# A 32-byte skew between operand chunks and weight slots in SBUF, in a two-block float32 network on one core

## The chip, the core and the metric

The kernel runs on one core of a Trainium2 chip. The metric is the device time of one execution in microseconds. Three timed executions of the kernel before gave 1040.45, 1042.25 and 1042.31 us; the median is 1042.25 us. [...]

## What is computed

Two transformer blocks follow each other on 256 tokens of 1,024 features, in float32. The first has a gated feed-forward layer, a mixer (neighbourhood attention on a grid, and pooling over windows), a second feed-forward layer and a gate; the second has a mixer (stick-breaking attention and a convolution), an attention over 256 memory tokens, and a third feed-forward layer. Nearly all arithmetic is in products of the 256 tokens with weight matrices:

```python
def swiglu(x, w_gate, w_up, w_down):
    return (jax.nn.silu(x @ w_gate) * (x @ w_up)) @ w_down
...
f = swiglu(rms_norm(h, ffn1_pre_g[i]), ffn1_w_gate[i], ffn1_w_up[i], ffn1_w_down[i])
h = h + 0.5 * rms_norm(f, ffn1_post_g[i])
m = hybrid_mixer(rms_norm(h, mix_pre_g[i]), w_in[i], rpb[i], pool_w[i], pool_scale[i],
                 w_br_attn[i], w_br_pool[i], w_out[i])
...
x = x + memory_cross_attention(rms_norm_2(x, norm_mem_q[l]), rms_norm_2(mem, norm_mem_kv[l]),
                               w_mem_q[l], w_mem_kv[l], w_mem_o[l])
hf = rms_norm_2(x, norm_ffn[l])
gate, up = jnp.split(hf @ w_ffn_in[l], 2, axis=-1)
x = x + (jax.nn.silu(gate) * up) @ w_ffn_out[l]
```

## The kernel before

**Tiles.** Features lie on partitions, tokens along the partition. An operand of 1,024 features is a tile of 8 chunks of 128 features, each chunk 256 float32 values (1,024 bytes) per partition. Every operand is held as two tiles of type float32r, a high part (H) and a low part (L), and every product of a 128 by 128 weight block with a chunk is three matmuls into the same PSUM bank (`mm3`, line 187): H chunk with high weights, H chunk with low weights, L chunk with high weights. The chunk (256 columns) is the moving operand, the weight block the stationary one. So the order on TensorE is, for each block, (xH, wh), (xH, wl), (xL, wh), and all of these matmuls carry the line of the helper, L184.

**Weights.** `Stream` (line 50) brings the weights in 345 units of 8 blocks, in the order in which TensorE takes them. A unit is 1,024 values (4,096 bytes) per partition. SyncE loads it into one of 5 slots of `raw`; ScalarE casts it into one of 7 slots of `wh` (line 90); VectorE subtracts that from `raw` into one of 6 slots of `wl` (line 101). `take` (line 105) hands out the blocks, 512 bytes apart within a slot.

**Stages.** Moving operands are `xH`, `xL` (the normed stream, 5,280 matmuls of 256 columns), `aH`, `aL` (22 chunks, the gated hidden layer of the three feed-forward layers, 1,584 matmuls), and smaller ones: `oH`, `oL`, `yH`, `yL` (branches of the mixers), `mH`, `mL` (memory), `x2H`, `x2L`, `moH`, `moL`, `pH`, `pL`. In the memory attention `xH` and `xL` hold the keys, `mvH` and `mvL` the values; they are filled from DRAM by GpSimd's transfers `kv` (line 1081). In the first products of each mixer (`first_group`) the weights move (512 columns) and slices of `xH` and `xL` are stationary.

**Order.** It is written out by hand: closures due after so many ticks (`after`, `tick`), generators of half tasks, and fillers for the norms. No scheduler moves anything.

**Places in SBUF.** Tiles stand one behind the other in the order in which the pools and tiles are made, in steps of 32 bytes. From the sizes in the code, counted in bytes within a partition: GpSimd's descriptor ring 0 to 16,384, then 128 bytes of constants, `hg` at 16,512, `xH` at 25,184, `xL` at 33,376, `fg`, then small tiles, `raw` from 52,032, `wh` from 72,512, `wl` from 101,184, `aH` at 141,536 and `aL` at 164,064; `mH`, `mL` (later `x2H`, `x2L`) from 212,960 up to the end. Slots of `wh` and `wl` are 4,096 bytes apart, blocks 512, chunks 1,024: all of them multiples of 512. So the place of an operand modulo 512 is the same for every chunk of a tile and for every weight block:

| operand | place mod 512 before | moving less stationary, mod 512 |
|---|---|---|
| every block of `wh`, `wl` | 320 | |
| `xH`, `xL` with weights | 96 | 288 |
| `aH`, `aL`, `oH`, `oL`, `yH`, `yL`, `moH`, `moL` with weights | 224 | 416 |
| `mH`, `mL`, `x2H`, `x2L` with weights | 480 | 160 |
| `xH`, `xL` (keys) with queries | 96 with 224 | 384 |
| `pH`, `pL` (probabilities) with `mvH`, `mvL` | 224 with 224 | 0 |

I call the last column the distance of a matmul's two operands. Lines that the change touches:

```python
h = self.hl.tile([P, UB * P], F32R, tag="wh", name="wh", bufs=HL_BUFS + 1)   # lines 73, 88
l = self.hl.tile([P, UB * P], F32R, tag="wl", name="wl")                     # lines 74, 100
self.xH = b.tile([P, DC, T], F32R, name="xH")                                # line 211
aH = fp.tile([P, FC, T], F32R, name="aH")                                    # line 409
nc = bacc.Bacc("TRN2", target_bir_lowering=False, num_devices=1)             # line 1402
```

## Time and profile before

| | |
|---|---|
| timed executions | 1040.45, 1042.25, 1042.31 us |
| span of the profiled execution, first to last instruction | 1040.2 us |
| what lies around the span, up to the median (the profiled execution has no time of its own beside its span) | 2.0 us |
| TensorE busy with matmuls | 1030.7 us (99%), 8,606 records |
| TensorE busy with weight loads | 1022.6 us (98%), 8,606 records |
| VectorE, ScalarE, GpSimd busy | 709.6, 545.7, 44.0 us |
| DMA queues: SyncE's, GpSimd's | 53.6% and 1.8% of 16 engines' span |

Matmul records overlap each other (one lasts 280 ns, the next starts some 117 ns later), so TensorE's busy time says little. What says how fast it goes is the distance from one start to the next. The chain of waits gives it: a piece "PE mm L184 xN" of so many microseconds is N matmuls that follow each other without a wait, and the quotient is the time that one takes.

### The profile page before, as it was taken

Reading aid. Unit: us, or ns where it says so; the run is one execution under the profiler, and the core shown is the slowest. Engines: PE = TensorE matmul, PEld = TensorE weight load, DVE = VectorE, ACT = ScalarE, POOL = GpSimd, SP = SyncE. Lnnn points to the kernel's source line nnn. Section 1 sums busy time; section 2 is a strip of 40 time slices with the busy share of each in tenths; the row PEclk is TensorE's granted clock in tenths of the full one; section 3 lists DMA queues with packets and bytes.
Section 4 is the critical chain, followed back from the end, with each engine's and each line's share of the span. In section 5 each row is a group of like instructions: output and inputs, shape, how many; then the busy total and the mean of one; then the engine's idle time right before and its main releaser. Section 6 shows DMA issues by size and latency. Waiting matters only on the chain.

```text
span 1040.2 us, 20720 instructions
## 1 busy us (share of the span) xinstructions
PE 1030.7 (99%) x8606; PEld 1022.6 (98%) x8606; DVE 709.6 (68%) x1062; ACT 545.7 (52%) x857; POOL 44.0 (4%) x73
## 2 busy tenths in 40 slices
PE   9999999999999999999999999999999999999997
PEld 8999999999999999999999999999999999999996
DVE  7777754587858677666447776886678677666642
ACT  7655544464644555454446565465556555544431
POOL 0100000120000110000000111000001000000000
PEclk9999999999999999999999999999999999999999
DMA  8765564555545655556555666454566346555541
GB/s 287 244 214 181 194 215 171 181 190 185 194 151 166 229 179 193 184 191 190 196 167 177 195 201 194 159 168 157 160 222 226 110 139 219 187 199 182 178 147 42
DMA packets 55023, 191.50 MB, mean 184 GB/s; under 512 B 6400, under 2 KB 7936, under 8 KB 54928
## 3 DMA queue, kind: packets, MB, share of 16 engines
q1 hardware_dynamic: 52992, 184.37, 53.6%
q0 software_dynamic: 1936, 5.80, 1.8%
q8 instruction: 67, 1.10, 0.4%
q14 instruction: 28, 0.23, 0.1%
HBM read 187.00 MB, written 3.15 MB: 183 GB/s over the span
## 4 chain that ended last, share of the span: by engine, by line
PE 81%; issue 16%; DMA 1%; DVE 1%; SPq 0%; POOL 0%; POOLq 0%; DVEq 0%; ACT 0%
PE mm L184 77%; PE at L184 3%; DMA raw<-ws 1%; PE at L839 1%; DMA hg<-gx 0%; DVE sqp L315 0%; POOL r L264 0%; DVE wl L79 0%; SPq L63 0%; DVE wl L101 0%; DVE xL L290 0%; DVE fg L1323 0%; POOLq L1405 0%; DVEq L1405 0%; ACT wh L78 0%
## 5 line engine op out<-in xcount | busy, mean ns | idle before, releaser
L184 PE MATMUL mm<-xH,wh 128*128 128x256 f32 x1760 | 494.9, 281 | 0.0
L184 PE MATMUL mm<-xH,wl 128*128 128x256 f32 x1760 | 492.2, 280 | 0.8 <-DVE wl L79 0.4
L184 PE MATMUL mm<-xL,wh 128*128 128x256 f32 x1760 | 491.4, 279 | 0.0
L101 DVE TENSOR_TENSOR wl<-raw,wh 128x1024 fp32r<-128x1024 f32 x340 | 405.8, 1218 | 22.0 <-ACT wh L90 7.4
L90 ACT CAST wh<-raw 128x1024 fp32r<-128x1024 f32 x340 | 350.2, 1046 | 53.0 <-PE mm L184 33.5
L184 PEld LDWEIGHTS mm<-xH,wl 128*128 128x128 f32 x1760 | 331.2, 188 | 2.6 <-DVE wl L79 1.4
L184 PEld LDWEIGHTS mm<-xH,wh 128*128 128x128 f32 x1760 | 331.3, 188 | 1.6 <-ACT wh L78 0.8
L184 PEld LDWEIGHTS mm<-xL,wh 128*128 128x128 f32 x1760 | 331.1, 188 | 0.0
L184 PE MATMUL mm<-aH,wh 128*128 128x256 f32 x528 | 148.9, 282 | 0.0
L184 PE MATMUL mm<-aL,wh 128*128 128x256 f32 x528 | 148.2, 281 | 0.0
L184 PE MATMUL mm<-aH,wl 128*128 128x256 f32 x528 | 148.2, 281 | 0.0
L415 ACT ACTIVATE z<-z 128x256 f32<-128x256 f32 x66 | 27.2, 418 | 145.6 <-DVE z L414 145.5
L184 PEld LDWEIGHTS mm<-aH,wl 128*128 128x128 f32 x528 | 99.6, 189 | 0.0
L184 PEld LDWEIGHTS mm<-aH,wh 128*128 128x128 f32 x528 | 99.6, 189 | 0.0
L184 PEld LDWEIGHTS mm<-aL,wh 128*128 128x128 f32 x528 | 99.5, 189 | 0.0
L414 DVE TENSOR_TENSOR z<-mm,rs 128x512 f32<-128x512 f32 x66 | 44.7, 689 | 77.5 <-PE mm L184 71.8
L305 DVE TENSOR_TENSOR acc<-acc,sq 128x256 f32<-128x256 f32 x27 | 11.5, 425 | 65.0 <-ACT sq L304 64.9
L264 POOL TENSOR_TENSOR r<-v,mhalf 128x2 f32<-128x2 f32 x13 | 17.6, 1355 | 685.7 <-DVE v L262 685.7
L286 ACT ACTIVATE xH<-hg 128x256 fp32r<-128x256 f32 x48 | 23.6, 543 | 31.9 <-DVE hg L355 22.0
L304 ACT ACTIVATE sq<-mm 128x256 f32<-128x256 f32 x21 | 8.2, 390 | 53.8 <-PE mm L184 53.8
L418 DVE TENSOR_TENSOR z<-z 128x256 f32<-128x256 f32 x66 | 27.2, 423 | 8.7 <-ACT z L415 7.5
L424 DVE TENSOR_TENSOR aL<-z,aH 128x256 fp32r<-128x256 f32 x66 | 26.6, 415 | 0.0
(238 smaller groups left out, 1225.9 us busy)
## 6 DMA issues: line engine op xcount, KB each, us to landing
raw<-ws SPq DMA_DIRECT2D x340, 512.0 KB, 4.1
raw<-ws SPq DMA_DIRECT2D x9, 256.0 KB, 6.0
ub<-ub SPq DMA_DIRECT2D x8, 160.0 KB, 2.9
mraw<-memT POOLq DMA_DIRECT2D x8, 128.0 KB, 3.7
kd<-kv POOLq DMA_DIRECT2D x8, 128.0 KB, 3.0
vd<-kv POOLq DMA_DIRECT2D x4, 256.0 KB, 3.4
kv<-kd POOLq DMA_DIRECT2D x4, 256.0 KB, 6.2
kv<-vd POOLq DMA_DIRECT2D x4, 256.0 KB, 7.1
```

Of the source, the lines that this page charges most:

```text
L90: self.nc.scalar.copy(out=h, in_=self.R[self.nhigh])
L101: self.nc.vector.tensor_tensor(out=l, in0=self.R.pop(u), in1=self.H[u].bitcast(F32), op=ALU.subtract)
L184: self.nc.tensor.matmul(out, lhsT, rhs, start=not b.started, stop=stop, skip_group_check=True)
L264: nc.gpsimd.tensor_tensor(out=r, in0=v, in1=self.mhalf, op=ALU.pow)
L286: self.nc.scalar.activation(out=self.ordered(x[0][:, c]), in_=self.rows(self.h[:, c]), func=AF.Copy, scale=gain(c))
L304: nc.scalar.activation(out=s, in_=in_, func=AF.Square, scale=scale)
L305: nc.vector.tensor_tensor(out=acc, in0=acc, in1=s, op=ALU.add)
L414: nc.vector.tensor_tensor(out=z, in0=b.t, in1=self.row(rs), op=ALU.mult)
L415: nc.scalar.activation(out=z[:, 0], in_=z[:, 0], func=AF.Silu)
L418: nc.vector.tensor_tensor(out=z[:, 0], in0=z[:, 0], in1=z[:, 1], op=ALU.mult)
L424: nc.vector.tensor_tensor(out=aL[:, m], in0=z[:, 0], in1=aH[:, m].bitcast(F32), op=ALU.subtract)
L839: self.nc.tensor.transpose(b.t[:, i * T + t * P:i * T + (t + 1) * P], u[:, t, kt * P:(kt + 1) * P], self.ident)
```

## The change

All of it is about places. A constant of 8 float32 values (32 bytes) is added to the distance between chunks of `xH`, `xL`, `aH`, `aL` (1,056 bytes instead of 1,024) and to the distance between slots of `wh` and `wl` (4,128 instead of 4,096). Only the first part of each is used, so what the engines read and write is the same size as before. Three small tiles of the base pool and `mr_keep` are made before `xH`, and three unused tiles (`pad0`, `pad1`, `pad2`) move what follows them. GpSimd's descriptor ring gets 8,192 instead of 16,384 bytes. Comments and docstrings are gone too.

The instructions of every engine stand in the same order as before. Eight of them change their shape: the four casts into `xH` and the four subtractions into `xL` that fill the keys of the memory attention (lines 1076 and 1077) work on two runs of 256 instead of one of 512.

```diff
+SKEW = 8
...
-        h = self.hl.tile([P, UB * P], F32R, tag="wh", name="wh", bufs=HL_BUFS + 1)
-        l = self.hl.tile([P, UB * P], F32R, tag="wl", name="wl")
+        h = self.high()
+        l = self.hl.tile([P, UB * P + SKEW], F32R, tag="wl", name="wl")[:, 0:UB * P]
...
+    def high(self):
+        return self.hl.tile([P, UB * P + SKEW], F32R, tag="wh", name="wh", bufs=HL_BUFS + 1)[:, 0:UB * P]
...
+        self.tmp.tile([P, 152], F32, name="pad1", bufs=1)
...
-        self.xH = b.tile([P, DC, T], F32R, name="xH")
-        self.xL = b.tile([P, DC, T], F32R, name="xL")
-        self.fg = b.tile([P, DC, T], F32, name="fg")
-        self.ident = b.tile([P, P], F32, name="ident")
         self.ones = b.tile([P, 1], F32, name="ones")
         self.mhalf = b.tile([P, 2], F32, name="mhalf")
         self.half = b.tile([P, 4 * DC], F32, name="half")
+        self.mr_keep = b.tile([P, 2], F32, name="mr_keep")
+        b.tile([P, 48], F32, name="pad0")
+        self.xH = b.tile([P, DC, T + SKEW], F32R, name="xH")[:, :, 0:T]
+        self.xL = b.tile([P, DC, T + SKEW], F32R, name="xL")[:, :, 0:T]
+        self.fg = b.tile([P, DC, T], F32, name="fg")
+        self.ident = b.tile([P, P], F32, name="ident")
...
-            aH = fp.tile([P, FC, T], F32R, name="aH")
-            aL = fp.tile([P, FC, T], F32R, name="aL")
+            aH = fp.tile([P, FC, T + SKEW], F32R, name="aH")[:, :, 0:T]
+            aL = fp.tile([P, FC, T + SKEW], F32R, name="aL")[:, :, 0:T]
...
+        edge = tc.tile_pool(name="edge", bufs=1, side="right")
+        edge.__enter__().tile([P, 248], F32, name="pad2")
...
-    nc = bacc.Bacc("TRN2", target_bir_lowering=False, num_devices=1)
+    nc = bacc.Bacc("TRN2", target_bir_lowering=False, num_devices=1, dynamic_dma_scratch_size=8192)
```

The places that follow, modulo 512 (c is the chunk, s the slot, both counted from 0):

| operand | before | after |
|---|---|---|
| `xH` / `xL` | 96 | 32c / 256 + 32c |
| `aH` / `aL` | 224 | 416 + 32c / 96 + 32c |
| `wh` / `wl` | 320 | 32s / 224 + 32s |
| `mH`, `mL`, `x2H`, `x2L` | 480 | 0 |
| `oH`, `oL`, `yH`, `yL`, `moH`, `moL`, `pH`, `mvH` and others of the stages | 224 | 416 |

## Rows read from the trace of the kernel before

**Rows 1.** The page: span, busy time of each engine, granted clock in 40 slices.
```profile
span 1040.2 us, 20720 instructions
...
PE 1030.7 (99%) x8606; PEld 1022.6 (98%) x8606; DVE 709.6 (68%) x1062; ACT 545.7 (52%) x857; POOL 44.0 (4%) x73
...
PEclk9999999999999999999999999999999999999999
```

**Rows 2.** The page: the chain that ended last, by engine.
```profile
PE 81%; issue 16%; DMA 1%; DVE 1%; SPq 0%; POOL 0%; POOLq 0%; DVEq 0%; ACT 0%
```

**Rows 3.** Groups by line: engine, operands, shapes, count, busy us, mean ns, idle before.
```profile
L184 PE MATMUL mm<-xH,wh 128*128 128x256 f32 x1760 | 494.9, 281 | 0.0
L184 PE MATMUL mm<-xH,wl 128*128 128x256 f32 x1760 | 492.2, 280 | 0.8 <-DVE wl L79 0.4 <-DVE wl L101 0.3
L184 PE MATMUL mm<-xL,wh 128*128 128x256 f32 x1760 | 491.4, 279 | 0.0
...
L184 PE MATMUL mm<-aH,wh 128*128 128x256 f32 x528 | 148.9, 282 | 0.0
...
L184 PE MATMUL mm<-yH,wh 128*128 128x256 f32 x68 | 19.4, 285 | 0.0
```

**Rows 4.** Chain in order of time, seven stretches: start us, us, engine and line, matmuls.
```profile
39.97 70.12 PE mm L184 x601
...
132.93 60.17 PE mm L184 x507
...
315.97 13.08 PE mm L184 x109
...
331.57 21.47 PE mm L184 x184
...
739.99 20.05 PE mm L184 x169
...
761.94 21.08 PE mm L184 x179
...
783.97 9.13 PE mm L184 x77
```

**Rows 5.** The same view in the memory attention: scores and products with values.
```profile
816.93 2.87 PE at L184 x24
```

**Rows 6.** Busy us (and count) of PE, PEld, DVE, ACT, POOL by stretch; granted clock.
```profile
40.00:110.00 70.00, 70.00 (x602) 70.00 (x602) 53.30 (x82) 39.29 (x68) 2.68 (x5) 1.00 0.61 200
133.00:193.00 60.00, 60.00 (x508) 60.00 (x507) 29.39 (x32) 27.48 (x38) 0.00 (x0) 1.00 0.58 196
316.00:329.00 13.00, 13.00 (x110) 13.00 (x110) 10.55 (x17) 6.03 (x10) 0.00 (x0) 1.00 0.52 172
```

**Rows 7.** Weight loads in the stretch 40:110 and in 316:329, columns as in rows 3.
```profile
L184 PEld LDWEIGHTS mm<-xL,wh 128*128 128x128 f32 x200 | 37.6, 188 | 0.0
...
L184 PEld LDWEIGHTS mm<-oL,wh 128*128 128x128 f32 x20 | 3.8, 191 | 0.0
```

**Rows 8.** PE in order of time in the first products of the first mixer: start us, us.
```profile
206.94 0.28 PE L184 MATMUL mm<-xL,wh 128*128 128x256 f32 x1
207.05 0.40 PE L184 MATMUL mm<-wh,xH 128*128 128x512 f32 x1
207.29 0.39 PE L184 MATMUL mm<-wl,xH 128*128 128x512 f32 x1
207.52 0.39 PE L184 MATMUL mm<-wh,xL 128*128 128x512 f32 x1
```

**Rows 9.** Groups of ScalarE and VectorE of two sizes each, columns as in rows 3.
```profile
L90 ACT CAST wh<-raw 128x1024 fp32r<-128x1024 f32 x340 | 350.2, 1046 | 53.0 <-PE mm L184 33.5 <-DMA raw<-ws 12.0 <-ACT wh L90 3.8
...
L311 ACT ACTIVATE sqp<-hg 128x512 f32<-128x512 f32 x28 | 17.0, 622 | 1.0 <-DVE sqp L315 1.0
...
L101 DVE TENSOR_TENSOR wl<-raw,wh 128x1024 fp32r<-128x1024 f32 x340 | 405.8, 1218 | 22.0 <-ACT wh L90 7.4 <-issue 7.1 <-PE mm L184 7.1
...
L315 DVE TENSOR_TENSOR sqp<-sqp 128x512 f32<-128x512 f32 x21 | 14.5, 690 | 6.5 <-ACT sqp L311 5.6
```

**Rows 10.** GpSimd's transfers: its queue on the page, and the tile kv between 740 and 830 us.
```profile
q0 software_dynamic: 1936, 5.80, 1.8%
...
kv<-kd POOLq DMA_DIRECT2D x4, 256.0 KB, 6.2
kv<-vd POOLq DMA_DIRECT2D x4, 256.0 KB, 7.1
...
  ACT mvH L1076: 0.7, 1
```

**Rows 11.** GpSimd's last kv transfer, and ScalarE's reading of it, in order of time.
```profile
797.35 0.72 POOL L1081 DMA_DIRECT2D kv<-vd  x1 [0.20 <-DVE r L1114]
...
811.26 0.62 ACT L1076 CAST mvH<-kv 128x512 fp32r<-128x512 f32 x1
```

## The prediction

> **What bounds the kernel now.** I read the page first. TensorE's matmuls are busy 99% of the span in every slice but the last and its granted clock is at the upper level throughout [rows 1]; the chain that ended last is TensorE for 81%, and 16% more is "issue", a stretch in which nothing that the profile shows was waited for and which holds the last feed-forward layer's matmuls [rows 2]. The groups by line say of what this consists: 3 x 1,760 matmuls with `xH` or `xL` moving, 3 x 528 with `aH` or `aL`, and some 1,300 smaller ones of the same size (the largest of those groups has 68), nearly without idle time before them [rows 3]. So no wait stands in the way; what counts is how far apart two matmuls start.

> The chain in order of time gives that distance. In the first feed-forward layer 601 matmuls on `xH`, `xL` take 70.12 us, 116.7 ns each. The next stretch, on `aH`, `aL`, has 507 in 60.17 us, 118.7 ns each. The branches of the first mixer take 13.08 us for 109, 120.0 ns; then `xH` again, 21.47 / 184 = 116.7 ns [rows 4]. It is the same instruction, on 256 columns, with a weight load of 128 columns beside it, and clock and load of the other engines do not explain the difference: the clock is 1.00 in all three stretches, and the slowest of them has ScalarE busy for 46% where the fastest has 56% [rows 6]. What differs is where the operands lie. `xH` and `xL` are at distance 288 from the weights, the others at 416 (see the table of places). The weight loads agree: 188 ns at distance 288, 191 ns in the slowest stretch [rows 7]. The distance is not all of it: at 288, the second mixer's last products take 21.08 / 179 = 117.8 ns, and at 416 there are 118.6 ns (20.05 / 169) as well as 120.0 [rows 4]. Something settles into one of several paces and stays there.

> **The change, part by part.** The instructions, their order and their waits are the same on every engine, so there is no term for added or removed work, and only the pace of a matmul can change.

> *The skew, for `xH` and `xL`.* Before, each of these 5,280 matmuls has the distance 288, the one with the best pace that is seen. Afterwards the distance walks by 32 bytes from chunk to chunk and from slot to slot, so that all 16 multiples of 32 below 512 turn up, each for three matmuls. Rows price four of them or their neighbours: 288 at 116.7 ns; 416 at 118.7, 120.0 and 118.6, mean 119.1; 160 (`x2H`) at 9.13 / 77 = 118.6 [rows 4]; 384 and 0 together (scores and products with values) at 2.87 / 24 = 119.6 [rows 5]. With one vote for each of these four entries the mean is 118.5. The other distances are priced by no row. I take for them the middle between the best pace, 116.7, and 118.5, which is 117.6, since a conflict of two read streams need not exist at every distance. With 4 of 16 at 118.5 and 12 at 117.6 the mean pace is 117.8. That is +1.1 ns for 5,280 matmuls, +5.8 us. Bounds: if all keep 116.7, 0; if all take the worst run's 120.0, +3.3 x 5,280 = +17.4 us.

> *The skew, for `aH` and `aL`.* From 118.7 to the same 117.8: -0.9 x 1,584 = -1.4 us (the last layer's 528 lie under "issue"; I give them the same pace). Bounds -2.0 x 1,584 = -3.2 and +1.3 x 1,584 = +2.1 us.

> *The slots, for the other 1,300.* Their own chunks stay 1,024 apart, but the weights' slots walk, so their distance does too: from about 118.6 to 117.8, -0.8 x 1,300 = -1.0 us; bounds -2.5 and +1.8 us.

> *ScalarE and VectorE.* They write and read the skewed tiles. A cast of 1,024 values takes 1,046 ns and an instruction of 512 takes 622, so 512 more cost 424 ns, 0.83 ns each; VectorE's 1,218 and 690 give 1.03 ns each [rows 9]. Before, `raw`, `wh` and `wl` all lie at the same place modulo 512, and still these two sizes of each engine, on different tiles, differ by little more than their lengths; I put the change at nothing. They are busy for 50 to 80% beside a full TensorE [rows 6], and that is the cover: even 10% more of the 1.2 us of a subtraction is 0.1 us for 24 matmuls (2.8 us). The eight keys' instructions in two runs are as long in elements: nothing.

> *The ring of 8 KB.* GpSimd's transfers make 1,936 packets in the whole run. The only ones in a hurry are the eight `kv`; they land 6.2 to 7.1 us after issue, and ScalarE waits 0.7 us in all for one [rows 10]. The last is issued at 797.35 and so lands by about 804.5, and is read at 811.26 [rows 11]: 6.8 us of cover. If a full ring made GpSimd wait for one landing (7.1 us), 0.3 us would show; I take 0, and 0 to +0.3.

> *The gathered tiles and pads* move `raw`, `fg` and `mH` only; nothing is bound there: 0.

> Sum: +5.8 - 1.4 - 1.0 = +3.4 us. I make it against the profiled execution, 1040.2 us of span and 2.0 around it up to the median of 1042.25: 1043.6 of span, **1046 us** to the nearest microsecond. Bounds of this case: from the evenly mixed 117.6 for everything (+4.8 - 1.7 - 1.3 = +1.8 us, 1044) to 118.6 (+10.0 - 0.2 + 0 = +9.8 us, 1052).

> [...]

> **The rivals.**

> *No change.* The pace could hang on something else than place, say on when a run of matmuls begins. For it: two paces at one distance (117.8 beside 116.7, and 118.6 beside 120.0) [rows 4]. Against it: the long runs on `xH` in all stages but one are at 116.7. Time 1042, within 1040 to 1044.

> *Everything at the best pace.* The slow paces need a distance that stays; with a distance that walks, none settles, and all matmuls take 116.7. For it: the paces look settled, one value over hundreds of matmuls. Against it: in the memory attention, where operands change most often, the pace is 119.6 [rows 5]. Price -3.2 (`aH`) - 2.5 (the others) - 0.2 (the 192 at 117.8) = -5.9 us: 1036, within 1033 to 1040.

> [...]

> [...]

> *The skew does not do what it says* would be a distance that stays; the places in the table exclude it for `xH`, `aH`, `wh` and `wl`.

> **How the numbers follow.** Slower by the mixed pace: 0.40. No change: 0.18. Everything at the best pace: 0.18. Well below it: 0.24. About 0.2% (2 us) is what a measurement of this kernel can tell from no change. Faster 0.42 (the last two), same 0.18, slower 0.40. The likeliest single case is the mixed pace: 1046, with its own range 1044 to 1052. Cases of both signs hold most of the chance, so the range reaches into the case far below: from 1000, which leaves out some 0.1 of it, to 1054, a little over the bound of the mixed pace, since its worst end (120.0 everywhere, +21 us) would need every distance to be as bad as one run of 109.

> **What would show it.** In the chain after: the 601 matmuls of the first feed-forward layer per matmul. Near 117.8 and no longer one fixed value: the mixed pace. 116.7 there and on `aH` too: everything at the best. [...] 116.7 and 118.7 as before: place modulo 512 does not matter. Wrong altogether would be a new wait on TensorE, a longer cast or subtraction at L90 and L101 (1,046 and 1,218 ns now), or GpSimd's `kv` transfers issued later relative to the scores.

## The result, and the profile after

The changed kernel takes 1048.68 us (median of three, 1048.51 to 1048.75) against 1042.25: a ratio of 1.0066, with a 95% interval from 1.0047 to 1.0086. It is slower by about 0.7%. The forecast was 1046, with 1044 to 1052 for its own case.

The page of the profile after (span, busy times, the chain that ended last by engine, the costliest groups, GpSimd's transfers):

```profile
span 1046.7 us, 20713 instructions
...
PE 1036.8 (99%) x8606; PEld 1029.1 (98%) x8606; DVE 710.0 (68%) x1062; ACT 545.4 (52%) x857; POOL 44.1 (4%) x73
...
PE 82%; issue 16%; DMA 0%; SPq 0%; DVE 0%; POOL 0%; POOLq 0%; DVEq 0%; ACT 0%
...
L189 PE MATMUL mm<-xH,wh 128*128 128x256 f32 x1760 | 498.0, 283 | 0.1
...
L105 DVE TENSOR_TENSOR wl<-raw,wh 128x1024 fp32r<-128x1024 f32 x340 | 406.0, 1219 | 20.5 <-issue 7.1
L91 ACT CAST wh<-raw 128x1024 fp32r<-128x1024 f32 x340 | 349.8, 1044 | 53.5 <-PE mm L189 34.2
...
kv<-kd POOLq DMA_DIRECT2D x4, 256.0 KB, 5.6
kv<-vd POOLq DMA_DIRECT2D x4, 256.0 KB, 6.6
```

TensorE is still busy for 99% of the span, with as many matmuls as before and nothing new to wait for [rows 1 to 3]. The cast and the subtraction take 1,044 and 1,219 ns (1,046 and 1,218 before [rows 9]), and `kv` lands in 5.6 and 6.6 us (6.2 and 7.1 [rows 10]). So the 6.5 us of span are in the pace of the matmuls. The chain in order of time, with a stretch of 720 on `xH`, `xL` first and then the stretches of rows 4 (start us, us, engine and line, matmuls):

```profile
30.17 85.24 PE mm L189 x720
...
39.98 70.10 PE mm L189 x592
...
133.98 61.05 PE mm L189 x516
...
316.94 13.10 PE mm L189 x111
...
332.90 22.21 PE mm L189 x188
...
744.93 20.13 PE mm L189 x170
...
766.00 22.08 PE mm L189 x187
...
788.43 9.68 PE mm L189 x83
```

Per matmul, against [rows 4]: `xH`, `xL` in the first feed-forward layer 118.4 ns (before 116.7), behind the first mixer 118.1 (116.7), in the second mixer's last products 118.1 (117.8). `aH`, `aL` 118.3 (118.7). The first mixer's branches 118.0 (120.0), the second's 118.4 (118.6), the memory queries 116.6 (118.6). Nearly everything has moved towards 118, from both sides, and `xH`, `xL` are by far the most.

By stretch (stretch; busy us and count of PE, PEld, DVE, ACT, POOL; granted clock; DMA share; GB/s):

```profile
40.00:110.00 70.00, 70.00 (x593) 70.00 (x593) 52.14 (x80) 38.60 (x66) 2.69 (x5) 1.00 0.63 198
134.00:195.00 61.00, 61.00 (x518) 61.00 (x518) 29.46 (x32) 27.47 (x38) 0.00 (x0) 1.00 0.62 196
```

In the same 70 us TensorE starts 593 matmuls where it started 602 [rows 6]; the clock is 1.00 as before, and VectorE and ScalarE do about 2% less in the same time.

### The profile page after: what moved, and what is told of

Its sections match the earlier page's. It is cut to its first block, busy times and chain, and to the rows that moved or that the text cites. A ratio compares the mean times of both kernels' runs of the same rounds, so it can differ in the third digit from the quotient of the medians.

```text
span 1046.7 us, 20713 instructions
## 1 busy us (share of the span) xinstructions
PE 1036.8 (99%) x8606; PEld 1029.1 (98%) x8606; DVE 710.0 (68%) x1062; ACT 545.4 (52%) x857; POOL 44.1 (4%) x73
## 3 DMA queue, kind: packets, MB, share of 16 engines
q0 software_dynamic: 1936, 5.80, 1.7%
## 4 chain that ended last, share of the span: by engine, by line
PE 82%; issue 16%; DMA 0%; SPq 0%; DVE 0%; POOL 0%; POOLq 0%; DVEq 0%; ACT 0%
PE mm L189 78%; PE at L189 3%; PE at L845 1%; DMA raw<-ws 0%; POOL r L271 0%; SPq L64 0%; SPq L229 0%; DVE fg L1331 0%; POOLq L1414 0%; DVE wl L80 0%; DVEq L1414 0%; ACT wh L79 0%; DVE v L269 0%
## 5 line engine op out<-in xcount | busy, mean ns | idle before, releaser
L105 DVE TENSOR_TENSOR wl<-raw,wh 128x1024 fp32r<-128x1024 f32 x340 | 406.0, 1219 | 20.5 <-issue 7.1
L91 ACT CAST wh<-raw 128x1024 fp32r<-128x1024 f32 x340 | 349.8, 1044 | 53.5 <-PE mm L189 34.2
```

Of the source, the lines that this page charges most:

```text
L91: self.nc.scalar.copy(out=h, in_=self.R[self.nhigh])
L105: self.nc.vector.tensor_tensor(out=l, in0=self.R.pop(u), in1=self.H[u].bitcast(F32), op=ALU.subtract)
```

## The experiments

Three theories stood at the start. D: the distance of moving operand and weights sets the pace; a fixed one gives one pace, a walking one the mean over distances. W: the walking itself breaks a steady rhythm. M: the place of the moving operand alone counts. All runs keep the whole computation. The first is the kernel before with the ring at 8 KB; all others start from that first one and differ from it in pads and strides only. Pads that keep the other tiles in place are left out of the diffs. "x" and "a" stand for `xH`, `xL` and `aH`, `aL`. Ratios are to the kernel before, run on the same chip, with 95% intervals. Rows are the chain of waits in order of time, as above; the stretch from 40 us on is x in the first feed-forward layer, that from 135 on is a there, that from 394 on is x in the second.

**The ring alone.**

```diff
+        b.tile([P, 2048], F32, name="padA", bufs=1)
         hg = b.tile([P, G_ALL + DC * T], F32, name="hg")
...
-    nc = bacc.Bacc("TRN2", target_bir_lowering=False, num_devices=1)
+    nc = bacc.Bacc("TRN2", target_bir_lowering=False, num_devices=1, dynamic_dma_scratch_size=8192)
```

> The kernel before, with GpSimd's descriptor ring at 8 KB and an unused tile of 8,192 bytes ahead of hg, so that every other tile stays where it was. All theories: no change, 1042 us within 2 us, 601 matmuls of the first feed-forward layer at 116.7 ns. If the ring itself costs anything, it shows here as more than 2 us or as a later landing of the eight kv transfers (6.2 to 7.1 us before).

1041.07 us, 0.9995 (0.9986 to 1.0005): no cost of the ring shows. One stretch differs though every operand lies where it did: `aH`, `aL` of the second layer go at 45.17 / 385 = 117.3 ns, where the kernel before has 45.09 / 380 = 118.7 in the same stretch (the second fence). So a distance can have more than one pace, and the places of the operands alone do not choose it.

```profile
39.90 70.11 PE mm L184 x601
...
499.94 45.17 PE mm L184 x385
```
```profile
499.91 45.09 PE mm L184 x380
```

**x at distance 416, all fixed.**

```diff
+        b.tile([P, 32], F32, name="padX", bufs=1)
         self.xH = b.tile([P, DC, T], F32R, name="xH")
```

> As the control with the small ring, but xH and xL lie 128 bytes further on; nothing walks. Their distance from the weights becomes 416 instead of 288 (modulo 512), that of aH, aL. D (a fixed distance sets the pace, and a walking one gives the mean over distances): the matmuls on xH, xL go from 116.7 to 118.7 to 119.1 ns, +10.6 to +12.7 us, 1053 to 1055. W (it is the walking itself that breaks a steady rhythm, whatever the distance): xH, xL stay at 116.7 and the time at 1042. M (the place of the moving operand alone matters): xH, xL then lie at 224 as aH does, so 118.7 and 1053 as with D.

1052.21 us, 1.0108 (1.008 to 1.0135). Chain, and the weight loads of the stretch 40:110 (count | busy us, mean ns | idle):

```profile
39.92 70.20 PE mm L184 x585
...
394.93 90.11 PE mm L184 x768
```
```profile
L184 PEld LDWEIGHTS mm<-xL,wh 128*128 128x128 f32 x195 | 37.2, 191 | 0.0
```

Nothing walks, and 128 bytes cost more than the whole change: 120.0 ns in the first layer, 117.3 in the second (118.9 over all of x, by the start times). W fails as the only cause; D and M had both asked for this. The weight loads have the 191 ns of rows 7.

**x and the weights moved together, so that all is at 288.**

```diff
+        b.tile([P, 32], F32, name="padX", bufs=1)
         self.xH = b.tile([P, DC, T], F32R, name="xH")
...
         self.mr_keep = self.base.tile([P, 2], F32, name="mr_keep")
+        self.base.tile([P, 32], F32, name="padR", bufs=1)
```

> xH and xL 128 bytes further on and the weights wh, wl also 128 bytes further on; nothing walks. xH, xL keep the distance 288 at another place (224 instead of 96), and aH, aL and the operands of the two mixers come from distance 416 to 288, with their places kept. D: xH, xL stay at 116.7 ns and the others come to 116.7 too: -2.0 x 1,584 - 2 to 3 x 800 = -5 us, 1037 to 1038. M: xH, xL go to 118.7 since they lie at 224, the others stay: 1053. W: no change, 1042.

1037.97 us, 0.9971 (0.9961 to 0.9981).

```profile
39.95 70.12 PE mm L185 x601
...
135.93 49.12 PE mm L185 x421
...
394.91 90.10 PE mm L185 x765
```

x lies where it lay in the run before and is back at 116.7; a has not moved at all and comes from 118.7 to 116.7, because the weights moved. That is D, and M fails. The gain is 3.6 us by the medians and not 5; in the profiled execution, which took 1039.47 us, x has 117.8 in the second layer, the pace that the second mixer had at this distance already [rows 4], and so has a there. The memory's operands, now at 32, have 116.7 to 117.8 too, so 32 and 288 are alike, as 160 and 416 were: the distance counts **modulo 256**. The later runs at fixed multiples of 32 bear this out, since the memory's operands lie 256 bytes further from the weights there than a does: by the start times both go, in their longest stretches, at 117.8 at 64 and 320, at 118.7 at 128 and 384, at 118.3 at 224 and 480, and both have 113.3 and 117.8 at 192 and 448.

**Only x walks; only the weights walk.**

```diff
-        self.xH = b.tile([P, DC, T], F32R, name="xH")
+        self.xH = b.tile([P, DC, T + 8], F32R, name="xH")[:, :, 0:T]
...
```
```diff
-        l = self.hl.tile([P, UB * P], F32R, tag="wl", name="wl")
+        l = self.hl.tile([P, UB * P + 8], F32R, tag="wl", name="wl")[:, 0:UB * P]
...
```

The first has the same line for `xL`, the second for `wh`.

> Only the chunks of xH and xL are 1,056 bytes apart; weights, aH, aL and all else lie where they did. D: over the 8 chunks of xH and xL the distance takes all 16 multiples of 32 below 512, as in the changed kernel: 118.0 to 118.9 ns for the 5,280 matmuls as there, +8 us, 1050; the others stay at 118.7 and 120.0. W: the same 1050, since the walk is there. M: the same. If instead the walk of the weights' slots is what costs, xH, xL stay near 116.7 and the time at 1042.

> Only the slots of wh and wl are 4,128 bytes apart; xH, xL, aH, aL lie as before, chunks 1,024 apart. D: within one weight block every distance is fixed for its matmuls, but from slot to slot and between wh and wl it takes all classes, so x goes to about 118.3 (+8 us), aH, aL to 118.3 (-0.5 us): 1050. If it is the walk of xH, xL alone that costs in the changed kernel, x stays at 116.7 and the time at 1042.

1046.68 us, 1.0049 (1.0034 to 1.0064), and 1048.37, 1.0060 (1.0045 to 1.0075). The x stretch of the first, then of the second:

```profile
40.00 70.05 PE mm L184 x592
```
```profile
39.94 70.13 PE mm L185 x593
```

118.3 ns in both, as the expectations have it; the times are 2 to 3 us under their 1050. Each part alone brings x to the pace of the changed kernel, and the two do not add up: a distance that walks already cannot walk more. The ratio of the second run, 1.0060, and that of the whole change, 1.0066, lie within each other's intervals. By the start times the intervals of x in the first run repeat every 24 matmuls (eight chunks, three each) between 114 and 123 ns, so a walk does not settle on one value; 118.3 is its mean.

**Six more fixed classes.** The same pads as in the run with all at 288, in other sizes: with k and j steps of 32 bytes ahead of x and of the weights.

```diff
+        b.tile([P, 8 * k], F32, name="padX", bufs=1)
...
+        self.base.tile([P, 8 * j], F32, name="padR", bufs=1)
```

> Fixed places again, other distances, counted modulo 256 from here on (288 and 32 gave the same paces, as did 416 and 160): xH, xL at distance 0 from the weights, aH, aL and the operands of the mixers at 64. D with classes modulo 256: each class has its own few paces; the mean over all eight multiples of 32 must come out near the 118.3 ns of the changed kernel, and as class 32 has 116.7 to 117.8 and class 160 117.3 to 120.0, the six others average 118.5: x near 118.5, time 1042 + 9 = 1051, within 1036 (another class as good as 32, or better) and 1062 (120.0 throughout). D modulo 512 would ask for a pace at 0 that differs from that at 256, which this run cannot tell. If only the mixture costs and no class does, x stays at 116.7 to 117.8, 1042 to 1047.

> xH, xL at distance 96 modulo 256, aH, aL and the mixers' operands at 128. D: x near 118.5 if this class is an average one, 1051; 120.0 if it is the worst, 1060; 116.7, 1041, if it is as good as 32. If the paces change smoothly with the distance, 96 lies between 32 (116.7 to 117.8) and 160 (117.3 to 120.0), so about 118.

> xH, xL at distance 192 modulo 256, aH, aL and the mixers' operands at 224. D: as the one before, 118.5 and 1051 for an average class; the three runs together with the two classes known must give a mean over the eight classes of 118.3 within 0.4 ns. If the paces change smoothly, 192 is near 160, 118 to 120, and 224 between that and 32.

1053.58 us, 1.0110 (1.0095 to 1.0126); 1058.27, 1.0160 (1.0143 to 1.0176); 1027.59, 0.9862 (0.9847 to 0.9876). For each run the x and the a stretch, and the weight loads of the first two in 40:110:

```profile
39.97 70.08 PE mm L185 x584
...
135.99 49.12 PE mm L185 x417
```
```profile
L185 PEld LDWEIGHTS mm<-xL,wh 128*128 128x128 f32 x195 | 37.4, 192 | 0.0
```
```profile
39.93 70.08 PE mm L185 x584
...
135.97 49.13 PE mm L185 x414
```
```profile
L185 PEld LDWEIGHTS mm<-xL,wh 128*128 128x128 f32 x195 | 36.6, 188 | 0.0
```
```profile
39.94 70.15 PE mm L185 x619
...
135.95 49.11 PE mm L185 x415
```

| distance mod 256 | paces seen, ns |
|---|---|
| 0 | 120.0 |
| 32 | 116.7, 117.8 |
| 64 | 117.8; 113.3 in the last layer's six stretches of 66 (start to start) |
| 96 | 120.0 |
| 128 | 118.7 |
| 160 | 117.3, 118.7, 120.0 |
| 192 | 113.3, 117.8 |
| 224 | 118.3 |

None of the three x stretches came out at the 118.5 of an average class: two are at 120.0 and one at 113.3, which nothing had pointed to. The mean over the eight classes is 117.2 with the lowest pace of each and 118.8 with the highest; the changed kernel's 118.1 to 118.4 lies between. With the mean pace of x or a over one whole run in each class (by the start times 119.9, 116.8, 116.6, 120.0, 118.7, 118.5, 114.2 and 118.3, from 0 to 224) it is 117.9, within the 0.4 ns that the expectation asked for. A small cost of the walking itself, some tenths of a nanosecond, is not excluded by that. The pace does not change smoothly, since 96 is worse than either neighbour. The mean duration of a weight load, 192 ns in class 0 and 188 in class 96, does not tell a slow class from a fast one: both run at 120.0. And two classes, 192 and in part 64, reach a pace far better than any of the kernel before.

**Between the multiples of 32.** x begins 16 bytes into its tile, and a too.

```diff
+        self.xH = b.tile([P, DC * T + 8], F32R, name="xH")[:, 4:4 + DC * T].rearrange("p (c t) -> p c t", c=DC)
```

> Distances between the multiples of 32: xH, xL at 208 modulo 256 and aH, aL at 176, the others at 160. If the class is set by blocks of 32 bytes, 208 behaves as 192 or as 224 (113.3 or 118.3) and 176 as 160 or 192. If the pace changes with every step, 208 and 176 give values of their own. At 113.3 for xH, xL the time is 1024 to 1028; at 118.3 it is 1050.

1054.26 us, 1.0123 (1.0106 to 1.0140): 119.2 ns for x at 208, and 119.2 for a at 176. Neither behaves as a neighbour, so the class is not set by blocks of 32 bytes. That the good class is narrow does not follow: both operands lie 16 bytes off the steps of 32 at which all other runs begin, both take the same 119.2, and no run has such a start at another distance. It may be the start itself that costs.

```profile
39.91 70.19 PE mm L185 x589
...
135.92 49.13 PE mm L185 x412
```

**Everything in class 192, at two sets of places.** In the first the moving operands lie at 224 and the weights at 32 modulo 256, in the second at 192 and 0.

> Everything at the class that was best for xH, xL: fixed places, xH, xL and aH, aL and the operands of mixers and memory attention at distance 192 modulo 256 from the weights (xH, xL at 224 instead of 192 modulo 256, so at another place than in the run that found the class). D: xH, xL as there, 113.3 to 117.8 ns with a mean of 114.2; aH, aL and some 800 others come from 118.3 to the same: -4.1 x 2,400 = -10 us from that run's 1027.6, so 1018, within 1015 (113.3 throughout) and 1030 (117.8 where the slower of the two paces settles). If place rather than distance made the 113.3, xH, xL lose it: above 1040.

> Class 192 for every family once more, but with the moving operands at place 192 and the weights at 0 modulo 256, as for xH, xL in the run that had 114.2 ns, and not at 224 and 32 as in the run that had 116.4. Class 192 has two paces, 113.33 and 117.78 ns; the question is what chooses. If the places themselves choose (192 and 0 give 113.33 more often), aH, aL and the 800 others come to 114.2 as well: 1027.6 - 4.1 x 2,400 = 1018, within 1015 and 1021. If the start of a stretch chooses, the part up to the first aH stretch repeats the earlier run (720 matmuls at 113.34), since nothing in it differs, and from there on each stretch takes one or the other anew: 1015 (113.3 in nearly all) to 1033 (as in the run with 224 and 32).

1033.24 us, 0.9920 (0.9905 to 0.9935), and 1030.25, 0.9893 (0.9876 to 0.9909): faster than before, but slower than the run that had only x there. The first lies outside its range of 1015 to 1030; the second lies where the start of a stretch was to choose. The x and a stretches of the first:

```profile
39.88 70.20 PE mm L185 x596
...
135.94 49.11 PE mm L185 x417
```

The second is shown from 28 us on, with the small matmuls ahead of its long stretch, and around the second layer's; below it stands the first long stretch of the run that had only x there:

```profile
29.45 0.44 PE at L185 x4
29.89 84.80 PE mm L185 x720
...
380.05 0.44 PE at L185 x4
380.50 164.54 PE mm L185 x1397
```
```profile
30.40 81.62 PE mm L185 x720
```

117.8 ns in the 720, though x and the weights lie exactly where they did in the run with 113.3. My expectation that these would repeat was wrong; neither the class nor the places of x and the weights settle which of the two paces is taken. What did differ just ahead of the 720 is the four matmuls of a broadcast, `ident` times `r`: `r` is in the pool of small tiles, which had moved by 32 bytes.

In both runs the 720 begin 31 ns after the last of these four. What differs first is the interval from the first of the 720 to the second: 206 ns in the run with 113.3, 201 here (it is this that the next expectation means by the 206 and 200 ns). In the four runs at class 192 (the next one included) this interval goes with the pace by the start times. Of the stretches of at least 16 matmuls at this class, 50 begin with 205 to 208 ns, and all of them went at 113.3 from the ninth interval on; 89 begin with 200 to 204 ns, and of these 53 went at 117.8 and 36 at 113.3. So a long first interval tells the pace, and a short one does not.

**The small tiles moved back.**

```diff
         self.tmp.tile([P, 72], F32, name="padT", bufs=1)
+        self.tmp.tile([P, 2], F32, tag="r16", name="r16", bufs=1)
```

The diff is against the run before. `r16` is a tile that this pool has already; made first, it puts the others 32 bytes further on, and the pool stays as long as it was.

> The run before with one change: the tiles of the small pool (sums of squares acc, the roots r and others) lie 32 bytes further on; every operand of the 256-column matmuls on xH, xL, aH, aL and of the weights lies exactly where it did. If the few small matmuls just ahead of a stretch choose between the two paces of class 192 by when they let it begin: in the run that had 114.2 ns acc and r lay at these places, and there the 256 columns after the broadcast ident x r began 206 ns after its last matmul and then went at 113.34; in the run before they began after 200 ns and went at 117.78. So the 720, 864 and 864 matmuls behind such a broadcast in the three feed-forward layers go at 113.3, -4.45 x 2,448 = -10.9 us, and the aH stretch of the second layer with them, -2.3: 1030.2 - 13 = 1017, within 1012 and 1022, while the 24 matmuls behind the sums ones x acc go at 117.8. If the small tiles have nothing to do with it, 1030 and the same stretches as before.

1015.96 us, 0.9763 (0.9749 to 0.9776), five executions from 1015.71 to 1019.25.

```profile
29.63 0.44 PE at L186 x4
30.07 81.62 PE mm L186 x720
...
376.62 0.44 PE at L186 x4
377.06 159.14 PE mm L186 x1404
```

81.62 / 720 = 113.4 ns and 159.14 / 1,404 = 113.3, where the run before had 117.8 twice. No operand of these stretches has moved; 32 bytes in the places of small tiles, which none of them reads, are worth 14 us. As expected, the 24 matmuls behind the sums now go at 117.8 (start to start). This kernel is 2.4% faster than the one before, and the best of all.

The whole pool moved, and ScalarE and VectorE read and write it too; that it is the operands of the four matmuls ahead of a stretch that count is argued from the order on TensorE and not shown by a run of its own. What the four runs at class 192 do show is that the place of the small tiles by itself does not choose either. In the first of the two runs above, with x at 224 and the weights at 32, the small tiles lie where they do in the run with only x at 192, and yet its 720 and both its 864 go at 117.8. Counted from `r`, x and the weights lie alike in those two runs that have everything at 192, and alike, 32 bytes lower, in the run with only x there and in this last one. The three long stretches begin with 200 or 201 ns and go at 117.8 in the first pair; they begin with 206 and go at 113.3 in the second. So it may be the distance from the small tiles that counts; two pairs do not prove it.

## Why the prediction came out as it did

**What bounds it** was right: the pace of the matmuls, which depends on places. The same instructions at other fixed places take 1015.96 us (the last run) to 1058.27 us (x at 96, a at 128). No other engine changed (VectorE busy for 709.6 us before and 710.0 after, ScalarE 545.7 and 545.4), and no wait but at the start, where 0.5 us went.

**The term for x** was mis-sized. I put it at +1.1 ns and +5.8 us. Over the some 5,170 intervals between two matmuls on x that are under 150 ns, the mean start to start goes from 116.76 to 118.24 ns: +1.5, times 5,280 is +7.8 us. The step that failed is the 117.6 that I took for twelve distances without a row, on the ground that a conflict of two read streams need not exist at every one; that there is such a conflict, no run here shows. The vote of the four priced entries, 118.5, which I had beside it, was nearer, in part by luck: 416 and 160, two of the four, are one class counted twice. The runs show why the middle was too low: the class of x was one of the three best of eight, and two others, 0 and 96, have 119.9 and 120.0 over a whole run. That 16 distances modulo 512 had to be told apart was also wrong; there are eight, modulo 256. Nor does each distance turn up for three matmuls, a whole block: by the table of places the three matmuls of a block have different distances after the change.

**The term for a** failed. I gave it -1.4 us; it is -0.2 (118.47 to 118.36 ns over 1,565 such intervals). The larger part of the miss is the same step: the walk goes at 118.4 and not at 117.8, which is 0.9 us. The rest, 0.4 us, is the 528 under "issue", which I gave the 118.7 of the first layer. By the start times half of them (four stretches of 66) went at 117.3 before, a lower pace of their class, and this layer lost about what the first gained (118.7 to 118.3).

**The other 1,300** and what remains: 6.5 - 7.8 + 0.2 = -1.1 us, where I had -1.0. By the start times all intervals but those on x and on a, from the first long stretch on, are 0.9 us shorter in sum. The first 720 begin at 30.17 us instead of 30.64 (before, below), which I had not foreseen, and what follows the last matmul is 0.6 us longer.

```profile
30.64 84.00 PE mm L184 x720
```

**The total** lies within its own case's 1044 to 1052: +3.4 us were forecast for the span and +6.5 measured. The mechanism, a mixed pace between those of the fixed distances, is what the runs show; its size was put at about half of what it is.

**The weight loads.** I read the 188 and 191 ns of rows 7 as agreeing with the paces. They do not follow them: 188 at 113.3 and, in class 96, at 120.0.

**Nothing for ScalarE, VectorE, the ring and the gathered tiles**: right, by the durations above (1,044 and 1,219 ns for the cast and the subtraction) and by the run of the ring alone (1041.07 us).

**The rivals.** "No change" held that the pace hangs on when a run of matmuls begins. That is a part of the truth: how a stretch begins goes with which pace of its distance it takes (at class 192 all 50 stretches that began with 205 to 208 ns went at 113.3), but the distance says which paces there are. "Everything at the best pace" rested on the paces looking settled. They are, and a walking distance does lose the fixed rhythm, but it then goes near the mean and not at the best (118.24 ns over all of x). The 0.24 for a pace well below the best, and the 1000 us at which the range begins for it, have no run behind them: no stretch of rows 4 goes under 116.7 ns. The runs showed such a pace, 113.3, at a fixed distance, 192 and in part 64, and not in the walk. None of the four priced entries had it, since neither 192 nor 64 was among them.

**What stays open**: why the distance counts modulo 256, why a class has two or three paces, and what chooses at the beginning of a stretch. Only multiples of 32 bytes and two distances between them were tried. Each kernel has one profile, so it is not shown that a kernel takes the same paces in every execution (those of x at 416 spread from 1050.15 to 1055.96 us, those of the last run from 1015.71 to 1019.25).

## What to carry to other kernels

When TensorE is busy throughout (99% of the span here) and one instruction form goes at several paces, divide the chain's stretches by their counts and set the paces beside the operands' places; here 32 bytes in the places of small tiles were worth 14 us (1030.25 to 1015.96). Look for a good fixed distance before spreading over all of them: the skew here came near the average (118.24 ns on x, where the mean over the eight classes is 117.9), a loss, since the place before had 116.76. Then check every long stretch for which of its paces it took, since here the places of small tiles that it does not read changed that (117.8 to 113.4 ns in the 720).
